# Feed forward's first projection: where the sums of weights are computed, and which tile holds A22

## The chip, the cores and the metric

The kernel runs on one core of a Trainium2 chip. A core has a TensorE (PE in the profile, with its weight loads as PEld), a VectorE (DVE), a ScalarE (ACT), a GpSimd (POOL) and a SyncE (SP), each with a queue of its own that it works off in order; here SP issues the DMAs. Matmuls write to PSUM, everything else lies in SBUF. The metric is the time on the device in microseconds (us), median of several runs.

## The reference

One layer of a hybrid encoder for 1024 tokens of a prompt and 8 x 16 tokens of samples, width 1024: an input projection, a gated linear recurrence and a sliding window attention beside it, an output projection, a cross attention into 256 memory tokens, and a SwiGLU feed forward of 2816 hidden features, each followed by a layer norm. The change is in the feed forward:

```python
def swiglu(x, w_in, w_out):
    g, u = jnp.split(x @ w_in, 2, axis=-1)
    return (jax.nn.silu(g) * u) @ w_out

x = layer_norm(ALPHA * x + swiglu(x, w_ffn_in, w_ffn_out), ln_g[2], ln_b[2])
```

All is float32. The kernel keeps that precision by splitting each operand into a high part (a cast to the matmul's type) and a low part (the rest), and multiplying high by high, high by low and low by high.

## The kernel before

The tokens are nine tiles of 128. Everything up to the memory attention goes in three groups of three tiles, until about 858 us of the profile. The feed forward goes in two units: the first of four tiles, the second of five.

`unit_operands` (L915) transposes a unit's rows and makes the seven operands of the products, in high and low parts: the B's, and the T's, which are differences that POOL computes (L933).

`hidden` (L943) computes two tiles of hidden features (a pair, below) for all of a unit's tokens, gate and up together. It goes by Winograd's form of Strassen's product. The weights of a pair are four blocks of 128 x 1024, A11, A12, A21 and A22, each loaded by one DMA. From them come four sums:

    S1 = A21 + A22    S2 = S1 - A11    S3 = A11 - A21    S4 = A12 - S2

Seven products follow, in this order: A11 B11, S1 T1, S2 T2, S4 B22, S3 T3, A12 B21, A22 T4. Each first splits its weights (`split`, L132 on ACT for the high part, L133 on DVE for the low part), then issues two times twelve matmuls (L93), and what comes out is copied (ACT, L968, L972, L977, L990) or added (DVE, L981, L984, L987) to the four tiles `m`. Then ACT and DVE form silu(gate) x up in `th` (L995 to L997) and split it to `h` (L1000, L1001).

`ffn` (L1003) runs the pairs of a part (of the 22 feature tiles: 6, 6, 4 and 6 in the first unit; 2 and five times 4 in the second), then `proj_rows` (L632) multiplies the part's `h` with the second projection's weights, and `add_rows` (L705, DVE) adds the result to the unit's rows. At a unit's end come the layer norms (L690 to L698, with one small operation on POOL, L692).

The order of the work is set twice. The Python classes `Order` and `TensorE` interleave the streams of work as they are emitted, by a clock of the products. Then a scheduler may let an instruction that is ready pass others, and hands out the buffers; a tile's buffer is free for the next when all that read it are done.

The buffers that matter here:

- `w_raw`, three of 128 x 1024: raw weights. A11, A21 and A22 of a pair lie here before the change, and the weights of every other projection. S3 is written over A11.
- `w_hi` and `w_lo`, four each: split weights. A split needs a free one of both, so it is at most three products ahead of TensorE.
- `temp(j)`: S1 (which S4 later overwrites), A12 and S2. In the first unit these are slots of the pool that also holds the unit's operands (16, of which the operands take ten; `th` takes one per pair). In the second unit S1 has a single tile of its own, and the others come from ten tiles named "big", which also hold the units' rows, the norms' weights and the first unit's `h`.
- PSUM: four banks "a" and four banks "b". The products with A11, S2, S3 and A22 add up in the same two banks "a".

In the kernel before, S1 (L970) and S3 (L975) are computed by POOL, S2 (L974) and S4 (L979) by DVE, and each sum is issued just behind the product that precedes its own.

Of the kernel before, what the change touches and what calls it, by code (L numbers as in the profile page):

```python
# [14 lines left out]
ALU = mybir.AluOpType  # L15
# [3 lines left out]
P = 128  # L19
# [4 lines left out]
GW = GT * P  # L24
# [4 lines left out]
FT = DFF // P  # L29
# the feed forward's units: first tile, tiles, parts of the hidden features' tiles  # L30
UNITS = ((0, 4, ((0, 6), (6, 12), (12, 16), (16, 22))),
# [3 lines left out]
TOK = NT * P  # L35
# tokens go in the order of ORDER: two tiles of the prompt, the samples (tile 8), the other tiles of the prompt
ORDER = (0, 1, 8, 2, 3, 4, 5, 6, 7)
# [5 lines left out]
class Event:  # L43
    """a point on TensorE's clock from which a result is expected to be there"""

# [4 lines left out]
class Order:  # L50
    """Order of emission. Streams are generators; one yields ns until its next step should find its operands ready,
    an Event to wait for, or None to go on. Of the streams that are ready, the one of the lowest rank goes on."""

# [25 lines left out]
class TensorE:  # L79
    """TensorE with the products' cost added to the clock of an Order"""  # L80

# [18 lines left out]
def trunk(ctx, tc, I, O):  # L100
    nc = tc.nc
    V, S, G = nc.vector, nc.scalar, nc.gpsimd
    order = Order()
# [34 lines left out]
    def raw_tile():  # L138
        return wp.tile([P, 1024], F32, name="w_raw", bufs=N_RAW)
# [21 lines left out]
    class Quads(list):  # L161
        """feature-major blocks [P, GW] in two parts, four to a slot"""

# [8 lines left out]
    def pair_slot(name):  # L172
        """two such blocks in one slot"""
        s = slot(name, F32R)
        return [(s[:, j], s[:, 2 + j]) for j in range(2)]
# [7 lines left out]
    def transpose_split(src4, dst, tcol):  # L183
        """four [P, P] blocks of src4, transposed, into dst [P, 4, .] at tcol in two parts"""
        split(transposes(src4).rearrange("p (a b) -> p a b", b=P), dst[0][:, :, tcol], dst[1][:, :, tcol])

    def spread(dst, src):
        """dst [P, 8, 32]: batch b's 16 columns of src [P, 128] at (b % 2) * 16, zeros elsewhere"""
        G.memset(dst, 0.0)
        s = src.rearrange("p (j e t) -> p j e t", e=2, t=16)  # L190
        d = dst.rearrange("p (j e) c -> p j e c", e=2)
        for e in range(2):
            V.tensor_copy(d[:, :, e, e * 16:e * 16 + 16], s[:, :, e])
# [9 lines left out]
    def fm(wsrc, x, which="a", n=GW, w=None):  # L203
        """one block of columns, feature major"""
        w = w or weights(wsrc)
        ps = bank(which)[:, :n]
        for kt in range(KT):
            mm3(ps, cut(w, ALL, cols(kt)), x[kt], kt == 0, kt == KT - 1)
            if kt % 4 == 3:
                yield  # L210
        return ps

# [1 line left out]
    ident = const.tile([P, P], F32, name="ident")  # L214
# [15 lines left out]

# [1 line left out]
    kv_dram = nc.dram_tensor("mem_kv_scratch", (4, P, 1024), F32, kind="Internal").ap()  # L232
# [36 lines left out]

# [1 line left out]
    mix_dram = nc.dram_tensor("mix_scratch", (8, P, TOK), F32, kind="Internal").ap()  # L271
# [95 lines left out]

# [1 line left out]
    def hgrn(g, h, xt, tm):  # L369
# [53 lines left out]
        def body():  # L423
# [7 lines left out]
            for t in range(npt):  # L431
# [5 lines left out]
                   px[0:64, 0:npt * 64].rearrange("p (j l) -> p j l", l=64))  # L437
            # from chunks to pairs of chunks
            V.tensor_tensor(half(kd, 0), half(kd, 0), wide(pl[:, 1:n64:2], 64), op=ALU.mult)
# [44 lines left out]
    def hgrn_sample(h, qg, kdt, v, at, pl, po, sv):  # L484
        """the sample's tile: a chunk and a state for each of its sequences"""
        c = cols(2)
# [22 lines left out]

# [1 line left out]
    def finish(sb, mx, sk, nk):  # L511
        """rows of sb [P, n, .]: exp(s - max), normalised with the sink's share"""
        n = sb.shape[1]
        zs, nm, e = small("zs"), small("nm"), small("e")
        V.tensor_scalar(nm[:, :n], mx[:, :n], -1.0, None, op0=ALU.mult)
        for i in range(n):
            S.activation(sb[:, i, :nk], sb[:, i, :nk], AF.Exp, bias=nm[:, i:i + 1], accum_out=zs[:, i:i + 1])
        V.tensor_tensor(e[:, :n], sk, mx[:, :n], op=ALU.subtract)
        S.activation(e[:, :n], e[:, :n], AF.Exp)
        V.tensor_tensor(zs[:, :n], zs[:, :n], e[:, :n], op=ALU.add)  # L520
        V.reciprocal(zs[:, :n], zs[:, :n])
        for i in range(n):
            V.tensor_scalar(sb[:, i, :nk], sb[:, i, :nk], zs[:, i:i + 1], None, op0=ALU.mult)

    def swa_tile(p1, ip, t, pos, q, ak, av):
        """heads 2 ip and 2 ip + 1 of both groups, one tile of queries over its own and the preceding tile of keys"""
        lt = pos % GT
# [102 lines left out]

# [1 line left out]
    def proj_rows(src, wsrc, evac, which, ahead=(), nt=GT, by_tile=False):  # L632
        """rows of nt tiles; src: blocks [P, nt * P] in two parts"""
        nk = len(src)
# [64 lines left out]

# [1 line left out]
    x2_dram = nc.dram_tensor("x2_scratch", (NT, P, D), F32, kind="Internal").ap()  # L701
# [44 lines left out]

# [1 line left out]
    def mem_heads(p2, st, g, ot, qf):  # L748
# [90 lines left out]
    def mem_sample(p2, qf, ot, ready):  # L839
# [5 lines left out]
        def cache():  # L845
            """the next part of the caches, four sequences to a tile"""
            src, h, part = parts.pop(0)
            out = []
            for bq in range(2):
                t = big("cache").rearrange("p (b m) -> p b m", m=256)  # L850
                nc.sync.dma_start(out=t, in_=I[src][h, part, :, bq * 4:bq * 4 + 4])
                out.append(t)
            loaded.append(out)
# [37 lines left out]

# [1 line left out]
    # The first projection goes by Winograd's form of Strassen's product: weights in halves of K and pairs of  # L893
    # feature tiles, tokens in halves (the first and the last 64 of each tile). With W = [A11 A12; A21 A22] and
    # x = [B11 B12; B21 B22]:
    #   S1 = A21 + A22, S2 = S1 - A11, S3 = A11 - A21, S4 = A12 - S2
    #   T1 = B12 - B11, T2 = B22 - T1, T3 = B22 - B12, T4 = B21 - T2
    #   U1 = A11 B11 + S2 T2, U2 = U1 + S3 T3
    #   C11 = A11 B11 + A12 B21, C12 = U1 + S1 T1 + S4 B22, C21 = U2 + A22 T4, C22 = U2 + S1 T1
    OPS = ("B11", "T1", "T2", "B22", "T3", "B21", "T4")  # L900
# [12 lines left out]
    def unit_operands(u):  # L913
        """a unit's rows, transposed, to the products' operands in two parts"""
        rows = [u.row() for _ in range(u.nt)]  # L915
# [27 lines left out]
    def hidden(u, i, temp, h):  # L943
        """two tiles of the hidden features of a unit's tokens; each weight tile holds gate and up"""
        def load(j, t):
            nc.sync.dma_start(out=t, in_=I["w_f1"][i, j])
            return t

        a11, a21, a22 = load(0, raw_tile()), load(2, raw_tile()), load(3, raw_tile())
        s1, a12, s2 = temp(0), load(1, temp(1)), temp(2)  # L950
        n = u.n
        X, Z, W = [], [], []
# [14 lines left out]
        for z in product(X, "a", a11, "B11", True):  # L967
            S.copy(m0[z][:, a], X[z][:, :n])  # L968
            yield
        G.tensor_tensor(s1, a21, a22, op=ALU.add)  # L970
        for z in product(Z, "b", s1, "T1", True):
            S.copy(m1[z][:, b], Z[z][:, :n])  # L972
            yield
        V.tensor_tensor(s2, s1, a11, op=ALU.subtract)  # L974
        G.tensor_tensor(a11, a11, a21, op=ALU.subtract)  # L975
        for z in product(X, "a", s2, "T2", False):
            S.copy(m0[z][:, b], X[z][:, :n])  # L977
            yield
        V.tensor_tensor(s1, a12, s2, op=ALU.subtract)  # L979
        for z in product(Z, "b", s1, "B22", False):  # L980
# [58 lines left out]

# [1 line left out]
    swa_bias = None  # L1041
# [30 lines left out]
    with tc.tile_pool(name="p1", bufs=1) as p1, tc.tile_pool(name="ps1a", bufs=1, space=PSUM) as pa, \  # L1072
            tc.tile_pool(name="ps1b", bufs=1, space=PSUM) as pb:
        pp["a"], pp["b"], pp["x"] = (pa, 3), (pb, 5), p1
        ak = tuple(p1.tile([P, 8 * P], F32R, name=f"ak{x}") for x in "hl")
        # of each head's values both parts side by side, the upper part in the columns of the head
        av = tuple(p1.tile([P, 8, P], F32R, name=f"av{x}") for x in range(2))
# [35 lines left out]
    def first_unit():  # L1113
        """fourteen blocks [P, 4, 256] in ten slots: the last two operands in the tails of the others' slots"""
        sl = [slot("x2", F32R).rearrange("p a c -> p (a c)") for _ in range(10)]
# [144 lines left out]
```

## Time and profile before

| | us |
|---|---|
| median of 3 runs | 1674.15 |
| lowest and highest run | 1671.29 and 1675.03 |
| span of the profiled execution | 1669.8 |
| first unit of the feed forward | about 858 to 1226 |
| second unit | about 1226 to the end |

The runs' times are of the device for the whole execution; the span goes from the first to the last instruction of one profiled execution. That execution's whole time isn't given beside its span; the median of the runs is 4.35 us above the span.

A profile's row has a line of the kernel, an engine, an operation, the tile that is written and those that are read, their shapes, a count, the busy time with the mean length of one, and the idle time of the engine just before with what ended it. "L133" is line 133 of the kernel; as a helper does every split, all splits stand under L132 and L133, with `w_raw` or `w_s` as what is split. A row of waits says which engine and line stood for which other, with the total, the number of times and the longest.

### The profile page before, as it was taken

What the parts mean: (1) busy time and instruction counts of PE and PEld (TensorE: products, weight loads), DVE (VectorE), ACT (ScalarE), POOL (GpSimd) and SP (SyncE); (2) the same over time, 40 slices, a digit from 0 to 9 for tenths busy, and PEclk for the clock granted to TensorE, in tenths of its full rate; (3) what the DMA queues carried; (4) which work ended last, traced back from release to release, by engine and by line L of the source; (5) the groups of instructions that cost most, each with busy time, mean ns of one, the idle gap of its engine ahead of it and who ended that gap; (6) DMA issues with size and microseconds to landing.
All of it is one profiled execution on the core that took longest, in us unless ns stands there. A gap on an engine that the chain in (4) does not pass through costs nothing. (4 is left out here: it accounts for less than half of the span.)

```text
span 1669.8 us, 26720 instructions
## 1 busy us (share of the span) xinstructions
PE 1618.8 (97%) x10341; PEld 1477.3 (88%) x10341; DVE 1235.5 (74%) x2161; ACT 735.8 (44%) x1471; POOL 244.2 (15%) x234
## 2 busy tenths in 40 slices
PE   8999999999999999999988999999989999999998
PEld 7998999999878987879878898989888999989896
DVE  6887688788568666787799577667898757566568
ACT  4543455445543555224645244345543424334241
POOL 1111121111000000000232110212232111111111
PEclk9999999999999999999999999999999999999999
DMA  7453343333884588646332523132543313131231
GB/s 244 128 179 125 93 151 102 105 115 108 277 313 149 169 274 311 234 138 227 101 114 91 176 89 127 64 101 91 175 168 122 101 58 107 51 101 64 89 100 65
DMA packets 84800, 233.65 MB, mean 140 GB/s; under 512 B 10048, under 2 KB 28352, under 8 KB 84672
## 3 DMA queue, kind: packets, MB, share of 16 engines
q1 hardware_dynamic: 84672, 231.93, 42.4%
q8 instruction: 81, 1.33, 0.3%
q14 instruction: 47, 0.39, 0.1%
HBM read 210.86 MB, written 20.97 MB: 139 GB/s over the span
## 5 line engine op out<-in xcount | busy, mean ns | idle before, releaser
L133 DVE TENSOR_TENSOR w_lo<-w_raw,w_hi 128x1024 fp32r<-128x1024 f32 (+1 forms) x279 | 343.1, 1232 | 166.4 <-ACT w_hi L132 165.5
L132 ACT CAST w_hi<-w_raw 128x1024 fp32r<-128x1024 f32 (+1 forms) x279 | 290.0, 1041 | 323.8 <-PE a L93 147.0
L93 PE MATMUL a<-w_hi,h 128*128 128x512 f32 x756 | 242.6, 394 | 5.2 <-DVE rows L705 2.6
L93 PE MATMUL a<-w_hi,q_hi 128*128 128x256 f32 (+1 forms) x576 | 197.0, 344 | 3.5 <-ACT w_hi L132 2.9
L93 PE MATMUL a<-w_lo,q_hi 128*128 128x256 f32 (+1 forms) x576 | 197.0, 342 | 1.9 <-DVE w_lo L133 1.8
L93 PE MATMUL a<-w_hi,q_lo 128*128 128x256 f32 (+1 forms) x576 | 195.4, 339 | 0.0
L93 PE MATMUL a<-q_hi,w_hi 128*128 128x384 f32 x528 | 186.8, 354 | 6.8 <-ACT q_hi L132 4.3
L93 PE MATMUL a<-q_hi,w_lo 128*128 128x384 f32 x528 | 180.1, 341 | 0.0
L93 PE MATMUL a<-q_lo,w_hi 128*128 128x384 f32 x528 | 179.9, 341 | 0.0
L93 PEld LDWEIGHTS a<-w_hi,h 128*128 128x128 f32 x756 | 141.8, 188 | 38.5 <-ACT h L1000 3.6
L132 ACT CAST w_hi<-w_s 128x1024 fp32r<-128x1024 f32 x88 | 92.2, 1048 | 181.3 <-PE a L93 87.9
L133 DVE TENSOR_TENSOR w_lo<-w_s,w_hi 128x1024 fp32r<-128x1024 f32 x88 | 134.6, 1533 | 35.9 <-ACT w_hi L132 35.9
L93 PE MATMUL a<-w_lo,h 128*128 128x512 f32 x378 | 148.2, 392 | 0.0
L970 POOL TENSOR_TENSOR w_s<-w_raw 128x1024 f32<-128x1024 f32 x22 | 54.8, 2492 | 490.6 <-DMA w_raw<-in_w_f_dram 428.7
L93 PE MATMUL a<-x,w_hi 128*128 128x256 f32 x704 | 126.3, 280 | 0.0
L93 PEld LDWEIGHTS a<-w_hi,q_hi 128*128 128x128 f32 x576 | 108.5, 188 | 17.9 <-ACT w_hi L132 3.3
L705 DVE SCALAR_TENSOR_TENSOR rows<-rows,a 128x512 f32<-128x512 f32 x123 | 82.7, 682 | 55.6 <-PE a L93 55.4
L93 PEld LDWEIGHTS a<-w_lo,q_hi 128*128 128x128 f32 x576 | 108.6, 189 | 16.8 <-DVE w_lo L133 3.4
L93 PEld LDWEIGHTS a<-w_hi,q_lo 128*128 128x128 f32 x576 | 108.6, 188 | 12.7 <-issue 0.5
L93 PEld LDWEIGHTS a<-q_hi,w_hi 128*128 128x128 f32 x528 | 100.6, 191 | 11.7 <-ACT q_hi L132 4.4
L93 PEld LDWEIGHTS a<-x,w_hi 128*128 128x128 f32 x704 | 108.1, 188 | 0.3
L93 PEld LDWEIGHTS a<-q_lo,w_hi 128*128 128x128 f32 x528 | 100.8, 191 | 1.9 <-issue 0.9
(247 smaller groups left out, 3662.5 us busy)
## 6 DMA issues: line engine op xcount, KB each, us to landing
w_raw<-in_w_f_dram SPq DMA_DIRECT2D x110, 512.0 KB, 3.6
w_raw<-in_w_fm_dram SPq DMA_DIRECT2D x41, 512.0 KB, 4.1
w_raw<-in_w_tm_dram SPq DMA_DIRECT2D x24, 512.0 KB, 3.6
w_raw<-in_w_out_dram SPq DMA_DIRECT2D x24, 512.0 KB, 5.4
w_raw<-in_w_mq_dram SPq DMA_DIRECT2D x24, 512.0 KB, 4.4
w_raw<-in_w_mo_dram SPq DMA_DIRECT2D x24, 512.0 KB, 4.1
w_s<-in_w_f_dram SPq DMA_DIRECT2D x22, 512.0 KB, 4.4
ln_gb<-in_ln_dram SPq DMA_DIRECT2D x16, 512.0 KB, 6.7
```

Of the source, the lines that this page charges most:

```text
L93: return self.eng.matmul(out, lhsT, rhs, **kw)
L132: S.copy(hi, src)
L133: V.tensor_tensor(lo, src, hi.bitcast(F32), op=ALU.subtract)
L705: V.scalar_tensor_tensor(y[t][:, hs], y[t][:, hs], scale, ps, op0=ALU.mult, op1=ALU.add)
L970: G.tensor_tensor(s1, a21, a22, op=ALU.add)
```

## The change

All four sums go to POOL. S1 and S2 are issued ahead of the first product, S4 behind the product of S1 (as S4 overwrites S1) and directly ahead of S3. A22 is loaded into a tile of the sums' pool, `temp(3)`, instead of a raw tile, so a pair takes two raw tiles and four of the pool. The comments and docstrings were taken out as well, with the numbers of lines kept up to this function.

```diff
-        a11, a21, a22 = load(0, raw_tile()), load(2, raw_tile()), load(3, raw_tile())
+        a11, a21, a22 = load(0, raw_tile()), load(2, raw_tile()), load(3, temp(3))
         s1, a12, s2 = temp(0), load(1, temp(1)), temp(2)
+        G.tensor_tensor(s1, a21, a22, op=ALU.add)
+        G.tensor_tensor(s2, s1, a11, op=ALU.subtract)
         n = u.n
...
         for z in product(X, "a", a11, "B11", True):
             S.copy(m0[z][:, a], X[z][:, :n])
             yield
-        G.tensor_tensor(s1, a21, a22, op=ALU.add)
         for z in product(Z, "b", s1, "T1", True):
             S.copy(m1[z][:, b], Z[z][:, :n])
             yield
-        V.tensor_tensor(s2, s1, a11, op=ALU.subtract)
+        G.tensor_tensor(s1, a12, s2, op=ALU.subtract)
         G.tensor_tensor(a11, a11, a21, op=ALU.subtract)
         for z in product(X, "a", s2, "T2", False):
             S.copy(m0[z][:, b], X[z][:, :n])
             yield
-        V.tensor_tensor(s1, a12, s2, op=ALU.subtract)
         for z in product(Z, "b", s1, "B22", False):
             V.tensor_tensor(m0[z][:, b], m0[z][:, b], Z[z][:, :n], op=ALU.add)
             yield
```

`temp` is handed in by the unit. In the first it is a slot for every j; in the second:

```python
lambda j: big("w_s") if j else c.tile([P, 1024], F32, name="w_s")
```

## The prediction

> **What bounds the kernel now.** I read the span and clock first, then the page's busy shares, then the feed forward in stretches, then who waits there, and last the instructions around one long wait.
>
> ```profile
> core 0: 1669.8 us, clock 0.993
> ...
> PE 1618.8 (97%) x10341; PEld 1477.3 (88%) x10341; DVE 1235.5 (74%) x2161; ACT 735.8 (44%) x1471; POOL 244.2 (15%) x234
> ```
>
> PE is busy for 97% of the span, so all that any scheduling change can win is in PE's gaps, about 51 us. This change touches the feed forward alone (from 858 us on):
>
> ```profile
> 858.00:1226.00 368.00, 350.57 (x2422) 325.73 (x2421) 280.60 (x331) 166.66 (x270) 77.69 (x48) 0.99 0.34 111
> 1226.00:1270.00 44.00, 36.79 (x206) 33.39 (x205) 42.91 (x58) 17.66 (x28) 11.64 (x8) 0.92 0.63 214
> 1270.00:1630.00 360.00, 360.00 (x2160) 337.12 (x2159) 233.36 (x266) 141.93 (x202) 45.67 (x19) 1.00 0.26 84
> ```
>
> The columns are the stretch, its length, busy PE, PEld, DVE, ACT and POOL, the granted clock, the DMA share and GB/s. The first unit (four tiles of tokens) lies in 858 to 1226 and leaves PE idle for 17.4 us; the entry of the second unit, to 1270, for 7.2 us. From 1270 to 1630 PE has no gap at all: there the change can win nothing. A product is 24 matmuls, in the first unit and in the second (rows of the chain of waits):
>
> ```profile
> 1016.93 2.85 PE a L93 x24
> ...
> 1278.62 3.52 PE b L93 x24
> ```
>
> A pair of feature tiles is seven products, so 20.0 us of PE in the first unit and 24.6 in the second. Who ended PE's waits, in the first unit and then behind it:
>
> ```profile
> PE b L93 <- DVE w_lo L133: 12.2, 10, 3.2
> PE a L93 <- DVE rows L705: 2.6, 2, 1.5
> PE a L93 <- DVE w_lo L133: 2.3, 2, 1.7
> ...
> PE b L93 <- DVE w_lo L133: 4.2, 1, 4.2
> PE a L93 <- ACT h L1000: 2.6, 2, 1.8
> ```
>
> So PE waits for the low parts of split weights. The two waits of bank "a" (2.3 us) are those of the first pair, the ten of bank "b" (12.2 us) those between one pair of feature tiles and the next. The timeline around the longest, POOL, DVE and PE in turn (start, length, then idle time before and its cause):
>
> ```profile
> 999.26 2.38 POOL L970 TENSOR_TENSOR w_s<-w_raw 128x1024 f32<-128x1024 f32 x1 [17.54 <-DMA w_raw<-in_w_f_dram]
> 1003.04 2.68 POOL L975 TENSOR_TENSOR w_raw<-w_raw 128x1024 f32<-128x1024 f32 x1 [1.39 <-ACT m L990]
> ...
> 991.49 1.22 DVE L133 TENSOR_TENSOR w_lo<-w_raw,w_hi 128x1024 fp32r<-128x1024 f32 x1
> ...
> 1001.68 1.22 DVE L974 TENSOR_TENSOR w_s<-w_s,w_raw 128x1024 f32<-128x1024 f32 x1 [3.15 <-POOL w_s L970]
> ...
> 1003.43 3.37 DVE L133 TENSOR_TENSOR w_lo<-w_s,w_hi 128x1024 fp32r<-128x1024 f32 x1
> ...
> 1006.85 0.58 PE L93 MATMUL b<-x,w_lo 128*128 128x256 f32 x1 [3.23 <-DVE w_lo L133]
> ```
>
> This is one chain. The next pair's A22 needs the last of three raw tiles, which falls free only when this pair's A22 is split (DVE, done at 992.71). POOL waits 17.54 us for that load, S1 comes at 999.26, DVE stands 3.15 us for it with everything queued behind S2, POOL then computes S3, and the split of S1 takes 3.37 us instead of 1.22 because it lies beside S3. PE waits 3.23 us. Its clock falls as well:
>
> ```profile
> 880.00:901.00 21.00, 18.21 (x143) 18.01 (x142) 19.02 (x21) 11.00 (x18) 3.13 (x2) 0.92 0.37 122
> 995.00:1018.00 23.00, 19.77 (x155) 19.57 (x154) 17.17 (x20) 11.50 (x19) 5.06 (x2) 0.93 0.23 84
> ```
>
> 0.08 of 21 us and 0.07 of 23 us are 1.7 and 1.6 us: two long waits cost 3.3 us beyond themselves.
>
> **The change, part by part.** *A22 in the sums' pool.* A pair then holds two of three raw tiles, so the next A11 loads at once and the next A21 as soon as S3 has been computed. In the first unit A22's slot is one of six (sixteen less ten of operands), of which a pair uses five: S1, A12, S2, A22 and `th`. The sixth takes the next A22. The last split of a pair thus no longer holds the load. It is the same number of loads on SP; only A22 and A12 can now stand there for a slot, with stores and second-projection weights behind them. In the first unit's raw tiles a load takes, from issue to landing:
>
> ```profile
> DMA to landing us min/median/max: 3.4/3.7/7.1
> ```
>
> That is short against a pair's 20 us, so I cost it at nothing; if SP did stand, each time would cost one load, 3.7 us.
>
> *Sums.* S2 and S4 go from DVE to POOL; S1 and S2 come ahead of the products.
>
> ```profile
> L974 DVE TENSOR_TENSOR w_s<-w_s,w_raw x11: 1209/1214/1225, 860.4 to 1163.3; 128x1024 f32<-128x1024 f32 x11
> L979 DVE TENSOR_TENSOR w_s<-w_s x11: 1210/1212/3107, 862.2 to 1171.3; 128x1024 f32<-128x1024 f32 x11
> L970 POOL TENSOR_TENSOR w_s<-w_raw x11: 2385/2403/3362, 877.5 to 1205.7; 128x1024 f32<-128x1024 f32 x11
> ```
>
> Per pair DVE loses 2 x 1.21 = 2.4 us and POOL gains 2 x 2.40 = 4.8 us, 9.6 in all of a pair's 20. POOL has the time. The Trainium skill ("GPSIMD Engine Reference", 4.1 Engine selection) speaks against the move: elementwise work with two inputs belongs on VectorE, being about twice as slow on GpSimd. The trace agrees on the ratio (2.40 to 1.21); that alone would cost 1.2 us a sum only where PE waits for one.
>
> What decides is the blocking. In the first unit's groups on DVE:
>
> ```profile
> L133 DVE TENSOR_TENSOR w_lo<-w_raw,w_hi 128x1024 fp32r<-128x1024 f32 x56 | 72.1, 1288 | 28.3 <-ACT w_hi L132 28.1
> L133 DVE TENSOR_TENSOR w_lo<-w_s,w_hi 128x1024 fp32r<-128x1024 f32 x44 | 68.8, 1569 | 13.8 <-ACT w_hi L132 13.8
> ...
> L996 DVE SCALAR_TENSOR_TENSOR th<-th,m 128x512 f32<-128x512 f32 x22 | 18.6, 846 | 4.2 <-ACT th L995 4.2
> L979 DVE TENSOR_TENSOR w_s<-w_s 128x1024 f32<-128x1024 f32 x11 | 15.3, 1388 | 0.1
> L997 DVE SCALAR_TENSOR_TENSOR th<-th,m 128x512 f32<-128x512 f32 x22 | 15.0, 682 | 0.1
> ...
> L984 DVE TENSOR_TENSOR m<-m,a 128x256 f32<-128x256 f32 x22 | 9.1, 416 | 2.4 <-PE a L93 1.8
> ...
> L696 DVE SCALAR_TENSOR_TENSOR rows<-rows,rs,ln_gb 128x512 f32<-128x512 f32 x4 | 4.8, 1197 | 0.0
> ```
>
> Against 1.22 for a split, 0.68 for `th` and 0.74 for a norm's row, the excess is 56 x 0.07 + 44 x 0.35 + 22 x 0.16 + 11 x 0.18 + 4 x 0.46 = 26.6 us, for 22 sums on POOL: 1.2 us of DVE's time per sum. Additions from PSUM (L984) don't stretch. DVE's own work for a pair is 7 splits, 6 `th` and 6 additions; splits in a row start 1.13 apart, so taking 0.08 off each: 7 x 1.13 + 6 x 0.60 + 6 x 0.33 = 13.5 us. Now: 13.5 + 2.4 + 2 x 1.2 = 18.3. After: 13.5 + 4 x 1.2 = 18.3. DVE's load stays, and DVE stays under PE, and the latency goes: S1 and S2 are there before their splits get a buffer of high and low parts (four of them, so a split can run three products, 8.6 us, ahead), and S4 has two products (5.7 us) for its 2.4.
>
> *What is late next.* Splits then queue behind one sum on POOL or behind `th`. The ten waits above hold several short ones, each of about half a microsecond; I leave one such, 0.5 us, at each of the seven changes of pair inside a part (eleven pairs in four parts): 3.5 us. Bounds: 0, and 2.2 each (a whole sum in front, 3.37 less 1.22), 15.4 us.
>
> *First pair.* Both sums wait for slots until the memory attention's last operands are read, about where they stand today; the 2.3 us stay (bounds 0 and 2.3 + 2.4).
>
> *Evacuation.* Two rows of the chain of waits:
>
> ```profile
> 1106.45 3.37 POOL w_s L970
> 1109.84 1.23 DVE w_s L974
> ```
>
> Of the 2.6 us for L705 the shorter wait (2.6 - 1.5 = 1.1 us, at 1111) comes from here: DVE stands for S1, with the evacuation queued behind S2. It goes. The longer one, with the second unit's operands, stays.
>
> *Entry of the second unit.* The rows of POOL, SP and DVE there:
>
> ```profile
> 1205.74 2.42 POOL L970 TENSOR_TENSOR w_s<-w_raw 128x1024 f32<-128x1024 f32 x1
> ...
> 1228.77 0.99 POOL L939 TENSOR_TENSOR T_l<-tt,T_h 128x256 fp32r<-128x256 f32 x1 [0.56 <-ACT T_h L938]
> ...
> 1222.42 0.33 SPq L946 DMA_DIRECT2D w_s<-in_w_f_dram  x1
> ...
> 1231.43 2.98 DVE L133 TENSOR_TENSOR w_lo<-w_s,w_hi 128x1024 fp32r<-128x1024 f32 x1
> ```
>
> Here A22 gets worse. Today its raw load is early and S1 is done at 1208; after, it waits for a "big" tile, and the first of these is free where A12 loads now, at 1222.4. Landed at about 1226, S1 stands ahead of or behind the last tile's sums, which end at 1229.8: it is done at 1228.5 or at 1232.2. Its split ends near 1231 or, behind S2, near 1236, against 1234.4 today. I take no change (bounds 3.4 us won, 4 lost with S3 also in front).
>
> *Second unit from 1270:* nothing. DVE has 24.6 us per pair.
>
> **The sum.** 12.2 (waits between pairs) + 3.3 (clock) + 1.1 (evacuation) - 3.5 (new short waits) = 13.1 us won. The span of the profile becomes 1669.8 - 13.1 = 1656.7. The three times have a median of 1674.15, 4.35 above that span; I take this to lie around it and to stay: **1661 us**, 0.8% faster. A measurement of this kernel can tell about 0.2% (3.3 us) from no change.
>
> **The rivals.** *Everything goes:* also the 3.5, the 2.3 and the entry's 4.2: 23 us won, 1651. For it: POOL is idle most of the time. Against: new neighbours on DVE.
>
> *The load isn't freed:* S1 comes as late as now, because its slots, or A22's and A12's on SP's queue, wait for `th` and S4 of the pair before. Five slots of six in use speak for it. Then only the evacuation's 1.1 us is won: 1673, within what can be told from none. The same time comes if new waits eat the gain.
>
> *The port (slower):* each POOL sum blocks DVE for all it can, 2.15 us (3.37 less 1.22), as S3 does nearly always now. The Trainium skill ("SBUF — State Buffer", Who interferes with whom) has this as a lock: a DVE instruction with two inputs in SBUF and a GpSimd instruction that reads SBUF exclude each other for a whole instruction. The trace agrees: the split that starts 0.39 us after S3 ends 1.08 us behind it. DVE then needs 13.5 + 4 x 2.15 = 22.1 us per pair, 2.1 over PE. Eleven pairs lose 23 us where 12.2 + 3.3 + 1.1 = 16.6 are lost now: 6 us slower, 1680. It decides from (20.0 - 13.5) / 4 = 1.6 us per sum on; 1.2 is measured. Against it: sums that are ready early needn't meet DVE's queue at its fullest.
>
> ```profile
> L996 DVE SCALAR_TENSOR_TENSOR th<-th,m 128x640 f32<-128x640 f32 x19 | 15.6, 821 | 4.2 <-ACT th L995 4.0
> ...
> L981 DVE TENSOR_TENSOR m<-m,b 128x320 f32<-128x320 f32 x20 | 9.7, 485 | 10.3 <-PE b L93 10.3
> ```
>
> Its place is the first unit. In the second, with these longer `th` and additions (0.08 off each again), 7 x 1.13 + 6 x 0.74 + 6 x 0.40 + 8.6 = 23.3 stays under 24.6.
>
> **How the numbers follow.** Forecast 0.62; everything goes 0.05; load not freed 0.17; port 0.16. Faster by over 0.2% is the first two, 0.67; within, 0.17; slower, 0.16. The forecast's own bounds (new waits 0 to 15.4 us, entry 3.4 won to 4 lost) run from 1654 to near 1677. Range 1650 to 1677: it takes in "everything goes" and no change, and leaves out the port's far end and a little below 1650.
>
> **What would show it.** Right: in the first unit PE's waits for `w_lo` fall from 14.5 to about 6 us; POOL's S1 no longer ends by a wait for the raw load; DVE never stands for S1; clock 1.00 in both stretches above; the evacuation's wait at 1111 is gone; 1270 on is as it was. DVE's busy time in the first unit stays near 281 us; if it rises by 10 or more, the port wins. Wrong would also be a longer wait at the second unit's entry, or gaps of PE behind 1270, by "big" tiles that the second unit's rows and A22 now share.

## The result and the profile after

| | before | after |
|---|---|---|
| median of the paired runs (4 each) | 1672.72 us | 1692.26 us |
| lowest and highest | 1669.42 and 1675.03 | 1689.34 and 1692.5 |
| ratio, 95% interval | | 1.0118 [1.0098, 1.0138] |

The change makes the kernel 1.2% slower; 0.8% faster was forecast. Span and clock after, and its busy shares:

```profile
core 0: 1690.3 us, clock 0.983
```

```profile
PE 1628.0 (96%) x10341; PEld 1486.0 (88%) x10341; DVE 1226.7 (73%) x2117; ACT 736.9 (44%) x1471; POOL 373.0 (22%) x278
```

POOL is now busy for 373.0 instead of 244.2 us, and DVE hardly less than before (1235.5 to 1226.7), though 44 sums left it. The granted clock fell from 0.993 to 0.983.

Where the 20.5 us of the span lie, by stretches of both kernels (length, busy PE, PEld, DVE, ACT, POOL, granted clock, DMA share, GB/s). The stretches begin at the first product, at the end of the first part's first projection, at the first unit's end, and behind the second unit's first part. Before:

```profile
858.40:927.10 68.70, 62.15 (x506) 61.09 (x506) 64.19 (x73) 34.89 (x56) 14.02 (x7) 0.98 0.37 116
927.10:1225.60 298.50, 287.63 (x1914) 263.91 (x1913) 216.00 (x258) 131.55 (x214) 62.87 (x40) 0.99 0.34 110
1225.60:1274.90 49.30, 42.09 (x229) 37.70 (x228) 47.44 (x64) 18.52 (x29) 12.64 (x10) 0.93 0.56 192
1274.90:1633.40 358.50, 358.50 (x2162) 336.58 (x2161) 232.20 (x264) 143.82 (x205) 45.08 (x19) 1.00 0.26 84
```

After:

```profile
861.00:941.30 80.30, 67.50 (x506) 66.25 (x505) 66.63 (x66) 35.88 (x57) 33.62 (x13) 0.89 0.28 94
941.30:1239.10 297.80, 287.67 (x1915) 264.52 (x1914) 215.14 (x242) 130.19 (x215) 109.04 (x56) 0.99 0.33 110
1239.10:1295.40 56.30, 45.22 (x229) 40.25 (x228) 48.38 (x59) 18.38 (x29) 27.45 (x14) 0.85 0.56 194
1295.40:1653.90 358.50, 358.50 (x2162) 336.60 (x2161) 220.57 (x247) 146.29 (x204) 94.18 (x36) 1.00 0.25 80
```

2.6 us come ahead of the first product, 11.6 in the first part, 7.0 at the second unit's entry; the rest of the first unit wins 0.7, and behind the entry nothing changes. In the two stretches that lose, busy PE grows too (62.15 to 67.50, 42.09 to 45.22) for the same matmuls: they run at a lower clock.

From the records of PE and of the clock, over the span from 835 us to 30 us before the end, I summed PE's idle stretches above 0.3 us, and the half of all half-clock time in which PE wasn't idle ("slowed"). Before: 28.9 idle and 5.6 slowed; after: 37.1 and 17.8. The span less both is 1635.3 and 1635.4 us. So of 20.5 us, 8.2 are waits and 12.2 are matmuls at half clock behind waits.

Who ended PE's waits in the first unit of after (total, times, longest):

```profile
PE b L93 <- DVE w_lo L133: 16.3, 8, 5.6
PE b L93 <- ACT w_hi L132: 4.4, 3, 2.1
PE a L93 <- ACT m L970: 2.0, 1, 2.0
```

Of the waits of "b", 1.8 us are the first pair's; 18.9 stand between pairs, where 12.2 stood and 3.5 were forecast. The timeline of one change of pair, POOL, ACT, DVE and PE:

```profile
1173.83 2.39 POOL L951 TENSOR_TENSOR w_s<-w_raw,w_s 128x1024 f32<-128x1024 f32 x1 [8.59 <-DVE m L984]
...
1176.30 2.73 POOL L952 TENSOR_TENSOR w_s<-w_s,w_raw 128x1024 f32<-128x1024 f32 x1
...
1177.13 2.44 DVE L997 SCALAR_TENSOR_TENSOR th<-th,m 128x512 f32<-128x512 f32 x1
1179.11 2.74 POOL L976 TENSOR_TENSOR w_raw<-w_raw 128x1024 f32<-128x1024 f32 x1
1179.61 0.62 ACT L1000 CAST h<-th 128x512 fp32r<-128x512 f32 x1 [1.57 <-DVE th L997]
1180.26 2.14 DVE L1001 TENSOR_TENSOR h<-th,h 128x512 fp32r<-128x512 f32 x1 [0.69 <-ACT h L1000]
...
1183.72 2.35 DVE L133 TENSOR_TENSOR w_lo<-w_s,w_hi 128x1024 fp32r<-128x1024 f32 x2
...
1184.99 0.38 PE L93 MATMUL b<-x,w_lo 128*128 128x256 f32 x1 [2.46 <-DVE w_lo L133]
```

S1 (L951) is ready at 1176.22, well ahead of its split, as meant. The split starts 7.5 us later, at 1183.72: it stands in DVE's queue behind `th` and `h` of the pair before, which go to and fro between DVE and ACT, and S2 and S3 (L952, L976) run beside just these. L997 takes 2.44 and L1001 2.14 us instead of 0.69. (S3 is issued behind the second product in both kernels, not just ahead of its own, the fifth.)

### The profile page after: what moved, and what is told of

It reads as the page before. It is cut to its first block, busy times and chain, and to the rows that moved or that the text cites. A ratio compares the mean times of both kernels' runs of the same rounds, so it can differ in the third digit from the quotient of the medians.

```text
span 1690.3 us, 26743 instructions
## 1 busy us (share of the span) xinstructions
PE 1628.0 (96%) x10341; PEld 1486.0 (88%) x10341; DVE 1226.7 (73%) x2117; ACT 736.9 (44%) x1471; POOL 373.0 (22%) x278
## 4 chain that ended last, share of the span: by engine, by line
PE 77%; DVE 10%; DMA 4%; issue 3%; ACT 2%; POOL 2%; SPq 0%; DVEq 0%; POOLq 0%; ACTq 0%
PE a L93 56%; PE b L93 19%; PE b L97 2%; DVE w_lo L133 2%; DVE th L997 1%; ACT w_hi L132 1%; DVE th L996 1%; POOL tt L933 1%; DMA w_raw<-in_w_fm_dram 1%; DMA w_s<-in_w_f_dram 1%; DVE h L1001 1%; DMA w_raw<-in_w_mv_dram 1%; DVE hg_a L405 1%; POOL w_s L951 1%; DVE sc L543 1%
## 5 line engine op out<-in xcount | busy, mean ns | idle before, releaser
L133 DVE TENSOR_TENSOR w_lo<-w_raw,w_hi 128x1024 fp32r<-128x1024 f32 (+1 forms) x257 | 320.3, 1249 | 154.3 <-ACT w_hi L132 152.8
L132 ACT CAST w_hi<-w_raw 128x1024 fp32r<-128x1024 f32 (+1 forms) x257 | 266.8, 1040 | 314.2 <-PE a L93 140.6
L132 ACT CAST w_hi<-w_s 128x1024 fp32r<-128x1024 f32 x110 | 115.0, 1051 | 221.8 <-PE a L93 121.2
L133 DVE TENSOR_TENSOR w_lo<-w_s,w_hi 128x1024 fp32r<-128x1024 f32 x110 | 147.1, 1343 | 76.8 <-ACT w_hi L132 76.5
L705 DVE SCALAR_TENSOR_TENSOR rows<-rows,a 128x512 f32<-128x512 f32 x123 | 82.9, 682 | 76.4 <-PE a L93 76.1
L951 POOL TENSOR_TENSOR w_s<-w_raw,w_s 128x1024 f32<-128x1024 f32 x22 | 57.9, 2630 | 336.4 <-DMA w_raw<-in_w_f_dram 132.5
L93 PEld LDWEIGHTS a<-w_lo,q_hi 128*128 128x128 f32 x576 | 109.3, 190 | 16.2 <-DVE w_lo L133 2.5
L93 PEld LDWEIGHTS a<-q_hi,w_hi 128*128 128x128 f32 x528 | 100.4, 190 | 11.6 <-ACT q_hi L132 4.8
L93 PE MATMUL b<-x,w_hi 128*128 128x256 f32 x528 | 102.8, 294 | 4.5 <-ACT w_hi L132 4.4
```

What stands on the lines that cost most here:

```text
L93: return self.eng.matmul(out, lhsT, rhs, **kw)
L132: S.copy(hi, src)
L133: V.tensor_tensor(lo, src, hi.bitcast(F32), op=ALU.subtract)
L705: V.scalar_tensor_tensor(y[t][:, hs], y[t][:, hs], scale, ps, op0=ALU.mult, op1=ALU.add)
```

## The experiments

Each row of this table is a profiled kernel: its median, its ratio to the kernel before on the same chip, the length of the stretches above, and idle and slowed as above, in us. There were several chips, on which the kernel before took 1671.87 to 1675.18 us; between kernels of different chips the ratios compare better than the medians. Stretches, idle and slowed are of one execution each.

| kernel | median | ratio [95%] | first part | rest of unit 1 | entry | idle | slowed |
|---|---|---|---|---|---|---|---|
| before | 1672.72 | 1 | 68.7 | 298.5 | 49.3 | 28.9 | 5.6 |
| after | 1692.26 | 1.0118 [1.0098, 1.0138] | 80.3 | 297.8 | 56.3 | 37.1 | 17.8 |
| e1 sums alone | 1697.78 | 1.0157 [1.0135, 1.0179] | 75.9 | 305.5 | 57.0 | 42.2 | 14.5 |
| e2 tile alone | 1685.55 | 1.0088 [1.0071, 1.0105] | 74.0 | 302.8 | 52.5 | 33.9 | 12.8 |
| e3 after, S2 and S4 on DVE | 1687.01 | 1.0084 [1.0065, 1.0104] | 75.6 | 304.4 | 52.5 | 34.2 | 17.4 |
| e4 after, raw A22 in unit 2 | 1693.66 | 1.0123 [1.0101, 1.0145] | 79.6 | 301.9 | 53.7 | 36.4 | 17.5 |
| e5 after, A22's load first | 1677.11 | 1.0014 [1.0001, 1.0028] | 76.2 | 290.0 | 55.2 | 28.8 | 11.0 |
| e6 after, S3 and S4 narrow | 1662.97 | 0.9934 [0.9919, 0.9948] | 68.1 | 286.1 | 55.3 | 20.4 | 10.3 |
| e7 before, no sum on POOL | 1651.93 | 0.9870 [0.9851, 0.9888] | 62.6 | 289.2 | 46.0 | 11.8 | 3.0 |
| e8 as e5, S3 on DVE | 1683.27 | 1.0060 [1.0036, 1.0084] | 74.9 | 296.6 | 55.7 | 30.9 | 11.7 |
| e9 as e7, idle sums on POOL | 1708.92 | 1.0222 [1.0204, 1.0239] | 84.1 | 325.6 | 46.0 | 53.6 | 22.1 |
| e10 tile, no sum on POOL | 1668.57 | 0.9983 [0.9970, 0.9995] | 68.0 | 295.5 | 48.9 | 18.7 | 7.4 |
| e11 as e10, A22's load first | 1664.16 | 0.9956 [0.9943, 0.9968] | 67.3 | 297.0 | 46.0 | 17.6 | 6.5 |
| e12 as e5, unit 2 plain | 1666.96 | 0.9965 [0.9947, 0.9982] | 76.4 | 289.9 | 46.0 | 22.1 | 10.0 |

The span of e1 and e4 has 3.7 us more behind the entry (398.6 instead of 394.9); all others are within 0.3 us of 394.9. The first product starts between 856.4 us (e6) and 861.8 us (e12), although no edit changes the work ahead of it.

**The change in halves (e1 to e4).** e1 is after with A22 back in a raw tile; e2 is before with only A22 in the sums' pool; e3 is after with S2 and S4 on DVE, at their new places; e4 is after with the raw tile in the second unit only. The edit shown is e1's.

```diff
-        a11, a21, a22 = load(0, raw_tile()), load(2, raw_tile()), load(3, temp(3))
+        a11, a21, a22 = load(0, raw_tile()), load(2, raw_tile()), load(3, raw_tile())
```

> Only A22 goes back to a raw tile; all sums stay on POOL, S1 and S2 ahead. Theory POOL (the sums in a row on POOL shut DVE's two-input work out and make S4 late): the first part of the first unit stays near 80 us (before 68.6, after 80.2) and the time stays above 1682; only the entry of the second unit (37.8 us, before 32.7) comes back. Theory tile (A22's load behind other loads on SP, or short of a slot, is the cause): within 4 us of the kernel before, 1673, with a first part of about 69 us.

> The kernel before with one edit: A22 in temp(3). S2 and S4 on DVE at their old places. Theory POOL: within 4 us of the kernel before in the first unit, the second unit's entry longer by about 5 us, 1673 to 1680. Theory tile: near the changed kernel, 1688 or more, first part near 80 us.

> The changed kernel with S2 and S4 back on DVE, at the changed places (S1 and S2 ahead, A22 in temp(3)). Theory POOL: 1673 to 1680, first part below 71 us. Theory tile: 1688 or more. If placement alone costs, it shows against e2, which differs from this kernel by the places only: theory POOL expects the two within 4 us.

> The changed kernel with A22 in temp(3) in the first unit and in a raw tile in the second. Both theories expect the second unit's entry back at about 33 us for its first pair and 16.6 for the projection behind it, so 5 to 7 us less than the changed kernel: 1685 to 1688. If the entry stays at 37.8 us, it is POOL's queue and not the tile that makes it late.

Measured: 1697.8, 1685.6, 1687.0 and 1693.7 us. Both halves cost by themselves (25 and 13 us), so no theory with one half as the cause holds, and without the two sums of e3 after's loss is smaller by 5 us only. None of the four forecasts was met in full: e1's entry didn't come back, e2 and e3 lie between the theories, and e4 is above its range. e3 differs from e2 by the places of the sums alone, and by 1.5 us, so the places in the order of issue cost little by themselves there. e4 brought nothing: the entry won 2.6 us, five parts behind it lost 0.75 each, and the rest of the first unit, whose code is after's, took 4.1 us more, 3.0 of them slowed time. In e1 the waits moved to bank "a", ended by ACT's copies of `m` (16.2 us in eight waits); I haven't followed that cause further. The next experiments go by mechanisms instead of halves.

**When the sums run (e5).** On SP, A22's load stands behind a raw load (after, rows of SP and DVE):

```profile
1168.83 0.33 SPq L143 DMA_DIRECT2D w_raw<-in_w_f_dram  x1
1169.21 0.90 SPq L946 DMA_DIRECT2D w_s<-in_w_f_dram  x2
...
1167.58 1.23 DVE L133 TENSOR_TENSOR w_lo<-w_raw,w_hi 128x1024 fp32r<-128x1024 f32 x1
```

The raw load needs S3's tile, which is free when S3 has been split (1168.81); A22 (the first of the two `w_s`) leaves SP 0.4 us later. e5 adds one edge to the order of issue: the next load of a raw tile stays behind A22's.

```diff
+    held = []
+    def behind(ins):
+        for x in held:
+            tc.add_manual_dep(ins.ins, x.ins.name, mybir.DependencyInfo(
+                mybir.DependencyClass.NoSync, mybir.DependencyReason.DATA), reason="order")
+        held.clear()
...
-            nc.sync.dma_start(out=t, in_=I["w_f1"][i, j])
+            ins = nc.sync.dma_start(out=t, in_=I["w_f1"][i, j])
+            if j == 0:
+                behind(ins)
+            if j == 3:
+                held.append(ins)
```

(`weights` calls `behind` on its load, too.)

> The changed kernel, with one thing forced on SP's queue: the load of a pair's A22 is issued ahead of the load that follows next in the raw tiles (the A11 of the pair behind, or the first weights of the second projection), where the changed kernel has it behind. Theory 'late load' (S1 comes at the end of a pair because its A22 stands on SP behind a raw load that waits for this pair's S3 to be split): S1 and S2 run some 4 to 8 us earlier, in the middle of the pair; the first unit's waits between pairs fall from 18.7 us to about 6, no clock stretch at half is left there (5 now, 27 us at half), the entry stays: about 1670. Theory 'port' (sums on POOL hold DVE's th and splits up wherever they lie): POOL still runs four sums per pair beside DVE, waits stay within 4 us of 18.7: 1685 to 1692.

Measured: 1677.1 us, between the two forecasts. By the medians 15 us are back; of the 17.2 us between the two profiled spans 4.1 lie ahead of the first product, so 13.1 are the feed forward's. In the first unit behind its first part, S1 and S2 now run early in a pair or in its middle (the pair of this S1 goes from 1142.8 to 1163.9), and PE's waits there follow below the row of S1:

```profile
1152.83 3.34 POOL L963 TENSOR_TENSOR w_s<-w_raw,w_s 128x1024 f32<-128x1024 f32 x1 [3.70 <-DVE w_lo L133]
...
PE b L93 <- DVE w_lo L133: 2.0, 2, 1.0
PE a L93 <- DVE m L996: 1.8, 2, 0.9
PE b L93 <- ACT w_hi L132: 0.6, 2, 0.3
```

4.4 us, against 10.0 in after in the same stretch. The first part keeps a wait of 4.6 us and its half clock, and the entry loses as before. POOL does as much as in after, so the place of its sums counts, not their amount alone.

**How much POOL does (e6, e7, e8).** e6 computes S3 and S4 of after for 64 of the 1024 columns and leaves out the rest; e7 is before with S1 and S3 on DVE; e8 is e5 with S3 on DVE. The edit shown is e7's.

```diff
-        G.tensor_tensor(s1, a21, a22, op=ALU.add)
+        V.tensor_tensor(s1, a21, a22, op=ALU.add)
...
-        G.tensor_tensor(a11, a11, a21, op=ALU.subtract)
+        V.tensor_tensor(a11, a11, a21, op=ALU.subtract)
```

> The changed kernel, with S3 and S4 computed for 64 of 1024 columns only (the rest is left out), so POOL works 5.2 instead of 10.7 us per pair; the loads and their order stay. Theory 'port': two of the four sums that block DVE are gone, S3 above all, which holds th and S1's split at the end of a pair (5.6 us at 896, 2.4 at 1023, 2.5 at 1185): waits between pairs fall from 18.7 us to 9 or less, 1692 becomes 1675 to 1680. Theory 'late load': S1 and S2 still come at the end of the pair and S1's split with them; waits fall by 3 us at most, 1686 to 1692.

> The kernel before, with S1 and S3 on DVE too, at their places: no sum on POOL. DVE's own time for a pair is 13.5 + 4 x 1.2 = 18.4 us, as now with the blocking counted. Theory 'port': no th and no split is stretched, S1 is done 1.2 us sooner and its split takes 1.2 instead of 3.4: the waits between pairs (12.2 us) and their clock (3.3 us) fall to about 3, so about 1660. Theory 'late load': A22 still lands when this pair's A22 has been split, S1 and its split still stand behind it; 1.2 us less at the two or three longest waits: 1667 to 1673.

> As the run with A22's load first, and S3 on DVE: three sums on POOL. Theory 'late load' alone: as that run, within 3 us, since nothing that PE waits for is left. Theory 'port': the S3 that lies beside th and S1's split is gone; 5 us or more faster than that run.

Measured: 1663.0, 1651.9 and 1683.3 us. e6 and e7 won more than either theory had forecast. e6 wins 29 us over after, with A22's load behind the raw load as there. e7 is the fastest of all, 1.3% under before, though DVE has 2.4 us more of its own per pair than before. The groups of DVE in the first unit, e7 first, then after:

```profile
L996 DVE SCALAR_TENSOR_TENSOR th<-th,m 128x512 f32<-128x512 f32 x22 | 15.1, 687 | 1.1 <-ACT th L995 1.1
L1001 DVE TENSOR_TENSOR h<-th,h 128x512 fp32r<-128x512 f32 x22 | 15.1, 686 | 2.7 <-ACT h L1000 2.7
L997 DVE SCALAR_TENSOR_TENSOR th<-th,m 128x512 f32<-128x512 f32 x22 | 15.1, 686 | 0.1
```

```profile
L133 DVE TENSOR_TENSOR w_lo<-w_s,w_hi 128x1024 fp32r<-128x1024 f32 x55 | 74.5, 1366 | 23.1 <-ACT w_hi L132 22.8
L133 DVE TENSOR_TENSOR w_lo<-w_raw,w_hi 128x1024 fp32r<-128x1024 f32 x44 | 58.9, 1339 | 23.5 <-ACT w_hi L132 23.0 <-DMA w_s<-in_w_f_dram 0.5
L1001 DVE TENSOR_TENSOR h<-th,h 128x512 fp32r<-128x512 f32 x22 | 34.8, 1580 | 7.5 <-ACT h L1000 7.5
L997 DVE SCALAR_TENSOR_TENSOR th<-th,m 128x512 f32<-128x512 f32 x22 | 27.6, 1256 | 1.1
L996 DVE SCALAR_TENSOR_TENSOR th<-th,m 128x512 f32<-128x512 f32 x22 | 21.6, 984 | 4.9 <-ACT th L995 4.9
```

Without sums on POOL a row of `th` or `h` takes 0.69 us and never more. After, the excess is 22 x (0.89 + 0.57 + 0.30) = 38.7 us on `th` and `h`, and with 1.22 for a split 55 x 0.146 + 44 x 0.119 = 13.3 on the splits. e8 missed both theories, being 6 us slower than e5. The sum that is left beside a split there is S4, and the wait has moved to bank "a":

```profile
991.34 2.73 POOL L987 TENSOR_TENSOR w_s<-w_s 128x1024 f32<-128x1024 f32 x1 [10.39 <-issue]
991.73 4.68 DVE L133 TENSOR_TENSOR w_lo<-w_s,w_hi 128x1024 fp32r<-128x1024 f32 x2
...
995.21 0.39 PE L93 MATMUL a<-x,w_lo 128*128 128x256 f32 x1 [1.30 <-DVE w_lo L133]
```

Two splits, S2's and S4's, take 4.68 us, where two that stand free take 2.35 (the row at 1183.72). It is the first, beside S4's sum, that is stretched, and PE waits 1.30 us for it.

**Sums that nobody waits for (e9).** Was it late results, or the blocking itself?

```diff
+        if u.nt == 4:
+            idle = temp(4)
+            for _ in range(4):
+                G.tensor_tensor(idle, a22, a22, op=ALU.add)
```

> The kernel before without sums on POOL (1652 us), with four additions of 128x1024 on POOL per pair of the first unit, A22 + A22 into a tile that nothing reads: no instruction waits for their results, only the next A22 load for their last read, which is over long before A22's own split. They run when A22 has landed, at the end of a pair. Theory 'port' (what costs is that a sum on POOL holds up th and the splits on DVE beside it): DVE's th and h rows rise from 0.69 to 1 us and more, the pair's end comes late, waits between pairs return: 1662 to 1675. Rival 'late result' (what costs is only that products wait for sums which POOL delivers late): within 3 us of 1652.

Measured: 1708.9 us. That is 57 us slower than e7, with no reader of any result, and more than twice the most (23 us) that the theory of the blocking had forecast. One change of pair of e9:

```profile
910.83 9.83 POOL L954 TENSOR_TENSOR w_s<-w_raw 128x1024 f32<-128x1024 f32 x4 [11.93 <-ACT m L994]
911.94 2.38 DVE L1000 SCALAR_TENSOR_TENSOR th<-th,m 128x512 f32<-128x512 f32 x1
914.24 2.38 DVE L1005 TENSOR_TENSOR h<-th,h 128x512 fp32r<-128x512 f32 x1
916.54 2.37 DVE L1001 SCALAR_TENSOR_TENSOR th<-th,m 128x512 f32<-128x512 f32 x1
918.84 2.91 DVE L133 TENSOR_TENSOR w_lo<-w_s,w_hi 128x1024 fp32r<-128x1024 f32 x1
...
921.80 0.58 PE L93 MATMUL b<-x,w_lo 128*128 128x256 f32 x1 [6.76 <-DVE w_lo L133]
```

While four sums run in a row on POOL, DVE gets exactly four operations through, one for one, whatever their own length: three of 0.69 and one of 1.22 us. That makes the four 6.75 us longer, and PE waits 6.76 us, so neither the slot that the idle tile takes nor A22's load is needed to explain this wait. In the first unit idle time goes from 3.8 us in e7 to 44.7, and slowed time from 0 to 20.5. The Trainium skill ("SBUF — State Buffer", Who interferes with whom) states the rule behind it, an exclusive lock for a whole instruction; the trace agrees, with 2.38 for 0.69.

**The tile without sums on POOL (e10, e11).** e10 is e2 with S1 and S3 on DVE; e11 adds e5's edge, and has the raw tile in the second unit.

> The kernel before with A22 in the sums' pool and all four sums on DVE at their old places: the tile's part of the change without any sum on POOL. If lateness of the load costs by itself, waits of about 2 us stay at most changes of pair, with half clock after them, as in the run with the tile alone (1685.6): 1668 to 1675. If the load's lateness only costs together with POOL's sums: the first unit as in the run without sums on POOL, the entry of the second unit some 7 us worse: 1656 to 1662.

> As the last, with A22's load ahead of the next raw load on SP, in the first unit only (the second has its raw tile back): both causes taken away, the tile kept. If early A22 is still worth something once POOL is out of the way: 1645 to 1650, below the 1652 of the run without sums on POOL. If not: 1650 to 1656.

Measured: 1668.6 and 1664.2 us, slower than e7 by 17 and 12 (by the ratios 1.1% and 0.9%). e10 lies in its first range, but for another reason, as PE's waits at the changes of pair are of 1.0 and not of 2 us; e11 is above both its ranges. So the tile won nothing even where nothing blocks, and in the first unit the forced order changes little (68.0 and 295.5 us against 67.3 and 297.0). By the traces S1's place in DVE's queue does a good part of the harm (e7, then e11 with DVE, ACT and PE):

```profile
970.61 1.22 DVE L970 TENSOR_TENSOR w_s<-w_raw 128x1024 f32<-128x1024 f32 x1
...
979.67 0.69 DVE L1008 SCALAR_TENSOR_TENSOR th<-th,m 128x512 f32<-128x512 f32 x1
980.27 1.22 DVE L982 TENSOR_TENSOR w_s<-w_raw,w_s 128x1024 f32<-128x1024 f32 x1
...
983.26 1.05 ACT L132 CAST w_hi<-w_s 128x1024 fp32r<-128x1024 f32 x1
...
984.36 0.73 PE L93 MATMUL a<-x,w_hi 128*128 128x256 f32 x4 [1.00 <-ACT w_hi L132]
```

A22 had been issued some 32 us before (at 948.64), yet the order made ahead of the run puts S1 (L982) into the midst of `th`, 20.9 us behind the part's first product; in e7 S1 (L970) stands ahead of `th`, 16.2 us behind that product. S2 comes later with it, ACT has S2's high part at 984.31 only, and PE waits 1.00 us for that. Of the 12.4 us by which e11's first unit is longer than e7's, 6.2 are idle and 3.4 slowed time; 2.8 stay open. Why the scheduler chose this order with the tile and not without it I haven't settled.

**The entry (e12).** e5, with the second unit as in e7.

> The run with A22's load first (1677 us) in the first unit; in the second unit A22 is back in a raw tile and all sums are on DVE at their old places. From the run before: its entry (first projection 37.1, second 18.1 us) should become that of the run without sums on POOL (31.9 and 14.1 us), so 9 us less, and the rest stay: 1665 to 1670. If the entry's loss has another cause (PE's clock from the gaps ahead, the norms of the first unit on DVE), 1674 or more.

Measured: 1667.0 us. The entry becomes 46.0 us, as in e7, and the other stretches stay as in e5. So the entry's loss is that unit's own.

## Why the prediction was wrong, point by point

- *"The last split of a pair thus no longer holds the load"*, with SP at no cost. Half right: inside a part S1 is ready 6 to 9.5 us ahead of its split, where it was 1.8 to 3.1 before. A good part of the added lead is the split's lateness: behind the first part, S1 comes only 1.0 to 4.1 us earlier than before, counted from the part's first product, and its split 2.8 to 4.4 us later; in the first part S1 itself comes 5.9 us later. The rival with a load that isn't freed was right in its half about SP's queue: SP's order put A22 behind a raw load, and S1 and S2 then fell on the end of a pair. The prediction had 3.7 us per such standing as a rival's price; what it cost was the place of the sums, 13 to 15 us (e5).
- **The step that failed** is *"DVE's load stays, and DVE stays under PE, and the latency goes"*. The size of the blocking was right: (38.7 + 13.3) / 44 = 1.18 us per sum, where 1.2 was taken. It was booked as load, spread over a pair's 20 us in which DVE has 1.7 to spare. It fell on a chain instead: three quarters of it on `th` and `h`, which S1's split queues behind. Before, `th` and `h` had 3.5 of 26.6 us. The load did stay, as DVE's busy time in the first unit went from 280.2 to 281.8 us only; so the prediction's own sign for the port, ten more, didn't show, and PE's waits grew all the same. e9 shows the chain alone: sums without a reader bring the waits back.
- *"Splits then queue behind one sum on POOL or behind `th`"*, 0.5 us each, at most 2.2: S2 and S3 run in a row, so two or three rows of `th` and `h` are held in turn (5.6 us at 896, 2.46 here). The bound assumed one sum.
- *"3.3 (clock)"* to be won: mis-sized with the wrong sign. Slowed time rose by 12.2 us and is the larger part of the loss.
- *First pair, "about where they stand today"*: the first pair's waits of 2.3 became 3.8 us (1.8 and 2.0), within the bounds. But the first part as a whole lost 11.6 us, by its rows 6.2 idle and 5.4 slowed, most of it by the wait of 5.6 at its first change of pair.
- *Evacuation, 1.1 us*: right. The wait at 1111 is gone (second projection of the third part 23.2 to 21.8 us).
- *Entry, "no change", 3.4 won to 4 lost*: 7.0 lost. A22 is issued where it was put, 13.5 us after 1222.42 in a kernel that is 13.5 us late there, but S1 stands on POOL behind the last tile's sums:

```profile
1235.88 1.01 SPq L946 DMA_DIRECT2D w_s<-in_w_f_dram  x2
...
1244.63 2.34 POOL L951 TENSOR_TENSOR w_s<-w_raw,w_s 128x1024 f32<-128x1024 f32 x1
...
1248.10 0.63 PE L93 MATMUL b<-T_h,w_hi 128*128 128x320 f32 x1 [5.34 <-ACT w_hi L132]
```

  By the rows of the stretches the entry's idle time grew by 3.9 us, the bound; the clock, not in the bound, took the other 3.1.
- *Second unit from 1270, "nothing"*: right, to 0.1 us. *The span's surroundings, 4.35 us*: 1.9 us (one execution took 1692.25 by the clock and 1690.3 by its span); small.
- *The port*, the rival on the slower side, had the right mechanism with the wrong measure. It was priced as DVE's load over PE's time, to decide from 1.6 us per sum. At 1.18 it had already decided, since a chain, not a load, was hit. The Trainium skill's word against the move ("GPSIMD Engine Reference", 4.1 Engine selection: elementwise work with two inputs goes to VectorE) holds here, by 1.3% from before to e7, though for the blocking rather than for the 2.40 against 1.21 us.

## What to carry to other kernels

Where POOL sums lie beside DVE work with two inputs in SBUF, charge each to the DVE instruction that stands beside it, at POOL's length, and ask whether that one is in a chain that PE waits for; the load of DVE over a stretch didn't show it here. Look for sums issued in a row at the change from one piece of work to the next. Using an idle engine isn't free: taking all sums off POOL won 1.3% over the kernel before.

## What the runs showed of the clock

In these traces half clock comes in windows of 3.41 us on a fixed grid. Two waits of 2.3 us show how it is decided. First e3, one stretch per window:

```profile
1156.30:1159.71 3.41, 1.08 (x8) 0.88 (x8) 3.41 (x2) 0.88 (x3) 1.84 (x1) 1.00 0.17 41
1159.71:1163.13 3.42, 3.42 (x18) 3.42 (x17) 2.70 (x4) 1.32 (x2) 0.00 (x0) 0.50 0.30 113
```

Then e2:

```profile
1152.78:1156.19 3.41, 1.61 (x14) 1.41 (x12) 3.41 (x2) 1.84 (x3) 2.70 (x1) 1.00 0.00 0
1156.19:1159.61 3.42, 2.88 (x24) 2.88 (x25) 3.36 (x4) 0.60 (x2) 0.00 (x0) 1.00 0.51 153
```

In e3 the wait falls into one window, 2.33 us of it idle, and the next runs at 0.50: 18 matmuls instead of some 30. In e2 the same wait is shared by two windows, 1.80 and 0.54, and the clock stays. Over the fourteen traces from 840 to 1640 us: of full-clock windows with 1.9 us idle or more, the next was at half in 64 of 64; between these and 0.8 it was mixed: in 6 of 7 with 1.75 to 1.9, in 4 of 96 with 0.8 to 1.75. At half, 0.48 us of idle time or more kept it there (42 of 42), less let it go (77 of 77). So, by these counts, a wait of 2 us costs 1.7 us more, or 3.4, or nothing, by where it falls; ten waits of 0.5 us cost 5, five of 2.4 cost 12 and their clock. That is also 2.0 of the 2.6 us ahead of the feed forward: the same wait of 2.9 us near 843 in both traces, half clock only after. Where such a wait lies on the grid isn't the change's doing, so this part of the difference between the two executions is chance.

The Trainium skill ("TensorE: Matmul & The Clock Gate", What's actually happening) has the half rate and a free-running window of 3413 ns, and the trace agrees with both. Where it speaks of an idle window, these runs have little more than half a window.
